# Layer norm behind a depthwise convolution: the last row tile is summed by TensorE on its own, without passing through the running sums

## The chip, the cores and the metric

The kernel runs on one core of a Trainium2 chip. The metric is the device time of one execution in microseconds (us); before the change the median of three runs was 1219.28 us.

## The reference, cut to what matters

One inference step of a small streaming encoder: 512 frames of a new stream and 64 frames of a running one, 576 columns of 1024 channels, all in f32. The first layer mixes time with a convolution module, the second with attention; each has a feed-forward part. The change lies in the convolution module:

```python
def conv_module(xn, prefix, w_in, b_in, w_dw, b_dw, ln_g, ln_b, w_out, b_out):
    a, gate = jnp.split(xn @ w_in + b_in, 2, axis=-1)
    u = a * jax.nn.sigmoid(gate)
    u_ext = jnp.concatenate([prefix.astype(u.dtype), u], axis=1)
    y = depthwise_conv(u_ext, w_dw) + b_dw          # 31 taps, each channel by itself
    y = jax.nn.silu(layernorm(y, ln_g, ln_b))
    return y @ w_out + b_out, u_ext[:, -CONV_STATE:]

def layernorm(x, g, b):
    mu = jnp.mean(x, axis=-1, keepdims=True)
    xc = x - mu
    y = xc * lax.rsqrt(jnp.mean(xc * xc, axis=-1, keepdims=True) + EPS)
    return y * g + b
```

The layer norm needs, for each frame, the sum of y and of its square over all 1024 channels.

## The kernel before, in words

Channels lie on the 128 partitions, time along the free dimension, so the 1024 channels are eight tiles. A column stretch of y has 608 elements (576 frames and the padding between the two streams).

The eight tiles are convolved in two ways. Tiles 0, 1, 2, 3 and 6 (`ROWS`) are *row tiles*: DVE and ACT with GpSimd apply the 31 taps (`conv`, line 1053); the last addition, line 1089, gives `y`. Tiles 4, 5 and 7 (`POLY`) are *polynomial tiles*: their input is stored to DRAM and read back spread over four phases of time (`vt`, line 935), TensorE multiplies it with band matrices (`wm`, loaded at line 938; the products `py` at line 942), DVE adds bias and shift (`ye`, line 952), and the result goes back through DRAM (lines 959 and 964). They work in the layout "p j n": four phases j of 152 columns n, where time is 4n + j.

The statistics of the layer norm are gathered in one PSUM tile, `cl` (two halves of 152 columns, for sum and sum of squares). For the polynomial tiles a matmul with `sum_of` adds up partitions. For the row tiles DVE keeps two running sums in the phase layout, `ys` of y and `sq` of the square (`add`, line 1095; the square by ACT, line 1101). Since a row tile has time in its natural order, these read y with a step of four floats (`in_phases`, line 1050). When the last row tile has been added, `rows_stat` lets TensorE add each running sum over the partitions with four matmuls with `sum_to`, one for each phase (`stat_rows`, lines 1002 and 998).

From `cl` come the square of the mean (`vs`, ACT, line 1211), the variance (DVE, lines 1212 and 1214), the negated mean `nmp` (ACT, line 1196), logarithm and exponential for the reciprocal root (`rs`, lines 1215 and 1216), and a Newton step on DVE that gives `rp` (lines 1217 to 1223). TensorE spreads mean and root over all partitions and back into the order of time (`nm` and `rt`, matmuls with `row_of`, line 1205). ACT copies `nm` for GpSimd (`nms`, line 1279). Then each tile is normalised: y plus mean (`zf`, line 1248), times root (line 1256), SiLU on ACT twice (`zh` rounded, line 1266, and in f32, line 1260), the rest `zl` (line 1270); the products `po` with the output weights follow (line 604). The output weights come by loads of 512 KB on SP's queue (`wr`, line 317). Matmuls of ones on nothing that is used (`warm`, line 794) keep TensorE's clock up in between; fourteen of them stand ahead of the layer norm's end.

The whole convolution module is one section of a planner (`Plan`, line 113). The code hands it operations in some order with an engine, an estimated cost, and what each reads and writes; it lists them by longest remaining path, with a preference for those marked urgent, and emits each engine's instructions in the order of the start times it found. So an edit of a few operations can move instructions of other engines, far from the edit.

Of the kernel before, what the change touches and what calls it, by code (L numbers as in the profile page):

```python
# [6 lines left out]
AF = mybir.ActivationFunctionType  # L7
# [3 lines left out]
P = 128  # L11
# [16 lines left out]
YW = UW - CS  # L28
# [11 lines left out]
QW = QN - Q0  # L40
# [9 lines left out]
ROWS = tuple(c for c in range(8) if c not in POLY)  # L50

KN = ROWS[:2]
# [60 lines left out]
class Plan:  # L113
# [19 lines left out]
    def op(self, eng, cost, fn, reads=(), writes=(), lat=0.0, group=None, bias=0.0, urgent=False, port=False):  # L133
        i, deps = len(self.ops), set()
        for k in reads:
            if k in self.w:
                deps.add(self.w[k])
            self.r.setdefault(k, []).append(i)
        for k in writes:
            deps.update(self.r.pop(k, ()))  # L140
            if k in self.w:
                deps.add(self.w[k])
            self.w[k] = i
        deps.discard(i)
        self.ops.append((eng, cost, fn, deps, lat, group, bias, urgent, port or eng == "Pool"))
        self.end.append(0.0)
# [75 lines left out]
def build(tc, xT, vec, st, stp, bdp, wt, ck, cv, w_in, w_out, gu, down, wk, wv, wq, wo, yT, csp, css, kp, ks, vp, vs):  # L222
    nc = tc.nc
# [88 lines left out]
    X = {}  # L312
# [32 lines left out]
    op = plan.op  # L345
# [8 lines left out]
    def tile(key, tag, shape, dt=F32, pool=None):  # L354
        X[key] = (pool or cur[0]).tile(list(shape), dt, name="_".join(map(str, key)), tag=tag)
        return X[key]
# [4 lines left out]
    def act(n, scaled=True):  # L361
        return 0.186 + n * 0.000834 if scaled else 0.16 + n * 0.000715

    def dve(n, ptr=False):
        return n / 960 + (0.13 if ptr else 0.07)
# [256 lines left out]
    class Norm:  # L622
# [7 lines left out]
        def add(self, c, e="Pool"):  # L630
            self.add_to(int(c == NC - 1), c in (0, NC - 1), c, e)
# [370 lines left out]
    def stat_rows(x, dep, i):  # L1002
        stat([((lambda j=j: sum_to[:, 96 - 32 * j : 224 - 32 * j]), (lambda j=j: x()[:, j, :])) for j in range(Q)], [dep], i)
# [46 lines left out]
    def in_phases(t):  # L1050
        return t.rearrange("p (n j) -> p j n", j=Q)
# [52 lines left out]

    def rows_sums(c):

        rows_done.append(c)
        a = rows_done[0]
        if c in KN[2:]:
            add(("ys",), "ys", ("y", c), ("y", c), True)  # L1110
        elif c == KN[1]:
            op("DVE", dve(YW), lambda: nc.vector.tensor_tensor(tile(("ys",), "ys", (P, Q, QW)), in_phases(X[("y", a)]), in_phases(X[("y", c)]), op=ALU.add), reads=[("y", a), ("y", c)], writes=["ys"], port=True)
        if c not in KN:
            add(("ys",), "ys", ("y", c), ("y", c), True)
            square(c)
        if c == ROWS[-1] and c not in KN:
            rows_stat()

    def rows_stat():
        a = ROWS[0]  # L1120
        stat_rows(lambda: X[("ys",)], "ys", 0)
        stat_rows(lambda: X[("sq", a)], "ysq0", 1)
# [45 lines left out]
    for e in events:  # L1168
        c = int(e[1:] or 0)
# [14 lines left out]
    def small(key):  # L1184
        return tile((key,), key, (P, QW))
# [26 lines left out]
    op("DVE", dve(QW, True), lambda: nc.vector.scalar_tensor_tensor(X[("vs",)], cl(1), 1.0 / D, X[("vs",)], op0=ALU.mult, op1=ALU.subtract), reads=sts, writes=["vs", "cl"], urgent=True)  # L1212
    op("ACT", act(QW) + 0.2, mean, reads=sts, writes=["nmp", "cl"], urgent=True)
    op("DVE", 0.08 + QW / 1920, lambda: nc.vector.tensor_scalar(X[("vs",)], X[("vs",)], 0.0, EPS, op0=ALU.max, op1=ALU.add), writes=["vs"], urgent=True, port=True)
    op("ACT", act(QW), lambda: nc.scalar.activation(small("rs"), X[("vs",)], AF.Ln), reads=["vs", "tbl"], writes=["rs"], urgent=True)
    op("ACT", act(QW), lambda: nc.scalar.activation(X[("rs",)], X[("rs",)], AF.Exp, scale=-0.5), reads=["tbl"], writes=["rs"], urgent=True)
    op("DVE", dve(QW), lambda: nc.vector.tensor_tensor(X[("vs",)], X[("vs",)], X[("rs",)], op=ALU.mult), reads=["rs"], writes=["vs"], urgent=True, port=True)
    op("DVE", dve(QW, True), lambda: nc.vector.scalar_tensor_tensor(X[("vs",)], X[("vs",)], -0.5, X[("rs",)], op0=ALU.mult, op1=ALU.mult), reads=["rs"], writes=["vs"], urgent=True, port=True)
# [1275 lines left out]
```

## Time and profile before

| | |
|---|---|
| median of 3 runs | 1219.28 us (1218.8 to 1220.41) |
| the profiled execution's own time | 1219.93 us |
| its span, first to last instruction | 1218.2 us |
| busy share of PE, DVE, ACT, GpSimd | 98%, 83%, 82%, 66% |
| granted TensorE clock | 0.995 of full speed |
| chain that ended last | PE 71%, DVE 11%, POOL 3%, issue 2%, ACT 2% |

Times in the profile count from the start of the span. PE is TensorE, DVE VectorE, ACT ScalarE, POOL GpSimd, SP the queue that sends the DMAs. A row of a timeline has the start, the length, the engine, the line, what is written and read, the shape, how many instructions are merged, and in brackets how long the engine stood idle before it and what ended that. An f32 matmul has two records in the trace.

### The profile page before, as it was taken

The page shows a single profiled execution, that of the slowest core. Times are in us where ns is not written, and L with a number is a line of the kernel's source. Part 1 is how long each engine was busy: PE and PEld are TensorE (multiplying, and loading weights), DVE is VectorE, ACT ScalarE, POOL GpSimd, SP SyncE. Part 2 cuts the span into 40 slices and gives each one's busy share as a digit, 9 for nine tenths or more (in the row PEclk, how much of TensorE's full clock was granted, in tenths as well). Part 3 has the DMA queues.
Part 4 walks back from the last instruction along what each step waited for, and adds up shares of the span by engine and source line. Part 5 has one row for each costly group of instructions (what it writes and reads, how often), then busy time and mean ns, then how long its engine had stood idle before and what let it go on. Part 6 is the DMA issues. An engine that isn't in the chain of part 4 may idle for free.

```text
span 1218.2 us, 23815 instructions
## 1 busy us (share of the span) xinstructions
PE 1190.0 (98%) x8670; PEld 1161.4 (95%) x8670; DVE 1016.9 (83%) x1643; ACT 998.1 (82%) x1887; POOL 808.6 (66%) x644
## 2 busy tenths in 40 slices
PE   9999989999999999999999999998999999999996
PEld 8999989999999999999999888998999999999996
DVE  6999987979996765998679999979799966668995
ACT  7988474799888887988659999955998889889983
POOL 1999823597867876996204554454699677789951
PEclk9999999999999999999999999999999999999998
DMA  7333822123133323323364322132232424224212
GB/s 270 90 94 93 263 67 86 52 92 117 53 122 105 104 70 94 115 70 106 118 160 105 74 62 74 53 104 59 81 121 71 121 71 122 87 70 123 86 70 78
DMA packets 44997, 121.07 MB, mean 99 GB/s; under 512 B 8784, under 2 KB 14224, under 8 KB 44880
## 3 DMA queue, kind: packets, MB, share of 16 engines
q1 hardware_dynamic: 44880, 119.56, 32.4%
q8 instruction: 68, 1.11, 0.4%
q14 instruction: 49, 0.40, 0.1%
HBM read 105.18 MB, written 5.70 MB: 91 GB/s over the span
## 4 chain that ended last, share of the span: by engine, by line
PE 71%; DVE 11%; POOL 3%; issue 2%; ACT 2%; DMA 1%; SPq 0%; DVEq 0%; POOLq 0%; ACTq 0%
PE j_A L1432 29%; PE j_B L1432 15%; PE j_C L1432 7%; PE po L604 4%; PE b L2226 3%; PE pw L604 3%; PE pq L604 3%; DVE wl L528 2%; DVE acc L1065 2%; PE b L2133 1%; PE av L2253 1%; PE pk L604 1%; DMA qd<-qd 1%; PE pd L604 1%; PE pg L604 1%
## 5 line engine op out<-in xcount | busy, mean ns | idle before, releaser
L518 ACT ACTIVATE wh<-wr 128x512 fp32r<-128x512 f32 (+1 forms) x295 | 178.9, 613 | 34.3 <-PE po L604 15.2
L528 DVE TENSOR_TENSOR wl<-S,hp 128x512 fp32r<-128x512 f32 (+1 forms) x258 | 169.4, 662 | 37.7 <-ACT hp L523 35.0
L528 DVE TENSOR_TENSOR wl<-wr,hp 128x512 fp32r<-128x512 f32 (+1 forms) x233 | 154.2, 666 | 43.2 <-ACT hp L523 39.4
L518 ACT ACTIVATE wh<-S 128x512 fp32r<-128x512 f32 (+1 forms) x260 | 155.7, 610 | 8.1 <-PE j_C L1432 2.9
L523 ACT ACTIVATE hp<-S 128x512 fp32r<-128x512 f32 (+1 forms) x258 | 148.6, 580 | 11.0 <-DVE wl L528 6.3
L523 ACT ACTIVATE hp<-wr 128x512 fp32r<-128x512 f32 (+1 forms) x233 | 134.3, 579 | 16.1 <-DVE wl L528 12.4
L448 POOL TENSOR_TENSOR S<-wr,wr 128x512 f32<-128x512 f32 (+1 forms) x65 | 87.7, 1349 | 86.1 <-ACT wh L518 32.1
L1082 POOL TENSOR_TENSOR pacc<-pacc,pr 128x608 f32<-128x608 f32 x69 | 109.0, 1592 | 7.3 <-ACT pr L1079 4.1
L484 POOL TENSOR_TENSOR S<-wr,S 128x512 f32<-128x512 f32 (+1 forms) x65 | 92.1, 1418 | 26.7 <-DVE wl L528 13.4
L448 POOL TENSOR_TENSOR S<-wr 128x512 f32<-128x512 f32 (+1 forms) x65 | 88.4, 1360 | 21.6 <-ACT wh L518 9.0
L448 POOL TENSOR_TENSOR S<-S,wr 128x512 f32<-128x512 f32 (+1 forms) x65 | 91.3, 1406 | 7.3 <-DVE wl L528 6.5
L1609 POOL TENSOR_TENSOR t<-t,r 128x576 f32<-128x576 f32 x44 | 69.0, 1572 | 3.5 <-ACT t L1580 2.3
L1609 POOL TENSOR_TENSOR a<-a,r 128x576 f32<-128x576 f32 x44 | 70.2, 1599 | 1.1 <-DVE a L1586 1.1
L1065 DVE SCALAR_TENSOR_TENSOR acc<-u,vecs,acc 128x608 f32<-128x608 f32 x76 | 64.6, 850 | 1.0
L1079 ACT ACTIVATE pr<-u,vecs 128x608 f32<-128x608 f32 x69 | 54.0, 795 | 8.3 <-POOL pacc L1082 8.0
L1615 DVE TENSOR_TENSOR a<-a,t 128x576 f32<-128x576 f32 x44 | 52.3, 1188 | 8.1 <-ACT t L1613 7.7
L1580 ACT ACTIVATE t<-j_A 128x288 f32<-128x288 f32 x84 | 34.1, 406 | 23.8 <-PE j_A L1432 22.7
L528 DVE TENSOR_TENSOR wl<-wr,wh 128x512 fp32r<-128x512 f32 x62 | 48.8, 797 | 4.1 <-ACT wh L518 4.0
L2226 PE MATMUL b<-s,sums 128*128 128x512 f32 (+1 forms) x196 | 48.4, 357 | 0.0
L1665 DVE TENSOR_TENSOR h<-j_A,h 128x288 f32<-128x288 f32 x92 | 41.2, 450 | 7.0 <-PE j_A L1432 6.6
L1989 POOL COPY qs<-q 128x64 f32<-128x64 f32 x8 | 3.3, 409 | 56.3 <-DVE q L1986 56.3
L1432 PE MATMUL j_A<-('x', 0, 0)_0_b,wh 128*128 128x288 f32 x168 | 35.7, 295 | 0.5 <-ACT wh L518 0.5
(987 smaller groups left out, 4541.0 us busy)
## 6 DMA issues: line engine op xcount, KB each, us to landing
wr<-gu SPq DMA_DIRECT2D x88, 512.0 KB, 3.6
wr<-down SPq DMA_DIRECT2D x32, 512.0 KB, 3.8
wr<-w_in SPq DMA_DIRECT2D x15, 512.0 KB, 3.9
wm<-wt SPq DMA_DIRECT2D x12, 576.0 KB, 6.3
wr<-down SPq DMA_DIRECT2D x16, 384.0 KB, 3.2
qd<-qd SPq DMA_DIRECT2D x21, 256.0 KB, 2.9
wr<-w_out SPq DMA_DIRECT2D x8, 512.0 KB, 3.8
wr<-wq SPq DMA_DIRECT2D x8, 512.0 KB, 3.6
```

The lines of the kernel that those rows point to most:

```text
L448: eng(e).tensor_tensor(t[:, :n], x[1](), y[1](), op=ALU.subtract if sub else ALU.add)
L484: eng(e).tensor_tensor(v[:, :n], X[("raw", i0)][:, n : 2 * n], v[:, :n], op=ALU.subtract)
L518: nc.scalar.activation(X[("w", u)][0][:, :n], get(), AF.Copy)
L523: nc.scalar.activation(t[:, :n], get(), AF.Copy)
L528: eng(le).tensor_tensor(b[:, :n], get(), a.bitcast(F32)[:, :n], op=ALU.subtract)
L604: nc.tensor.matmul(o[hf], (hi, hi, lo)[j][:, s], (xh, xl, xh)[j], start=(start and q == 0 and j == 0), stop=(stop and q == n - 1 and j == ...
L1065: nc.vector.scalar_tensor_tensor(dst, src, wt_, dst if i else X[("kneg",)], op0=ALU.mult, op1=ALU.add)
L1079: nc.scalar.activation(tile(("pr", c, i), f"pr{m}", (P, YW)), src, AF.Copy, scale=wt)
L1082: nc.gpsimd.tensor_tensor(X[("pacc", c)], X[("pacc", c)], X[("pr", c, i)], op=ALU.add)
L1432: nc.tensor.matmul(out, a[:, s], b, start=(start and q == 0 and i == 0), stop=(q == len(ops_) - 1 and i == 2), skip_group_check=True,)
L1609: nc.gpsimd.tensor_tensor(X[k], X[k], r, op=ALU.mult)
L2226: nc.tensor.matmul(out(zz()), X[(w,)], get(x), start=False, stop=(i == len(mms) - 1), skip_group_check=True)
```

## The change

When the last row tile (6) comes, the running sums of the four earlier row tiles are handed to TensorE as they are. Tile 6 gets eight matmuls of its own: four on y, whose operand is y read with a step of four floats, and four on its square, which ACT now writes in the natural order of time (contiguous in and out, marked urgent), read with the same step by TensorE. DVE's two additions for tile 6 are gone. Besides, the planner is told that the logarithm waits for the mean.

```diff
     def rows_sums(c):
 
+        if c == ROWS[-1] and c not in KN:
+            rows_stat()
+            stat_rows(lambda: in_phases(X[("y", c)]), ("y", c), 0)
+            op("ACT", act(YW, False), lambda: nc.scalar.activation(tile(("sq", c), "ysq1", (P, YW)), X[("y", c)], AF.Square), reads=[("y", c)], writes=["ysq1"], urgent=True)
+            stat_rows(lambda: in_phases(X[("sq", c)]), "ysq1", 1)
+            return
         rows_done.append(c)
...
-        if c == ROWS[-1] and c not in KN:
-            rows_stat()
...
-    op("ACT", act(QW), lambda: nc.scalar.activation(small("rs"), X[("vs",)], AF.Ln), reads=["vs", "tbl"], writes=["rs"], urgent=True)
+    op("ACT", act(QW), lambda: nc.scalar.activation(small("rs"), X[("vs",)], AF.Ln), reads=["vs", "nmp", "tbl"], writes=["rs"], urgent=True)
```

Lines after the edit count four more in the changed kernel than before. Behind the convolution module the order of every engine is as it was; within it the planner moves instructions on all engines. Three places matter.

On PE, the sums `cl` between the products of the last polynomial tile and the spreading of the mean. Before (`yes`, and the first `sq` with `sum_of`, are the sums of tiles 4 and 5; `ye_7` and `sq_7` those of tile 7; `ys` and `sq_1143` the running sums of the row tiles):

```order
L998 MATMUL cl<-yes,sum_of 128x152
L998 MATMUL cl<-sq_1737,sum_of 128x152
L998 MATMUL cl<-ye_7_0_1876,sum_of 128x152
L998 MATMUL cl<-sq_7_0_1882,sum_of 128x152
L794 MATMUL warm<-ones 128x128 x2
L998 MATMUL cl<-ye_7_1_1895,sum_of 128x152
L794 MATMUL warm<-ones 128x128 x2
L998 MATMUL cl<-sq_7_1_1908,sum_of 128x152
L794 MATMUL warm<-ones 128x128 x2
L998 MATMUL cl<-ys,sum_to 128x152 x4
L998 MATMUL cl<-sq_1143,sum_to 128x152 x4
L794 MATMUL warm<-ones 128x128 x8
```

The same place on PE in the changed kernel (`y_1900` is tile 6, `sq_1910` its square, `sq_1151` the running sum of squares):

```order
L998 MATMUL cl<-yes,sum_of 128x152
L998 MATMUL cl<-ys,sum_to 128x152 x4
L998 MATMUL cl<-sq_1151,sum_to 128x152 x4
L998 MATMUL cl<-y_1900,sum_to 128x152 x4
L998 MATMUL cl<-sq_1910,sum_to 128x152 x4
L998 MATMUL cl<-sq_1735,sum_of 128x152
L998 MATMUL cl<-ye_7_0_1876,sum_of 128x152
L998 MATMUL cl<-sq_7_0_1882,sum_of 128x152
L998 MATMUL cl<-ye_7_1_1896,sum_of 128x152
L998 MATMUL cl<-sq_7_1_1908,sum_of 128x152
L794 MATMUL warm<-ones 128x128 x7
```

The sums of the row tiles now stand ahead of five sums of the polynomial tiles, and seven of the fourteen warming matmuls are left ahead of `nm`; the other seven stand behind `rt`.

On SP's queue, around the moment when the input of tile 7 is read back (`vt_1735`, `vt_1738`) and its bands are loaded (`wm`). Before:

```order
L938 DMA wm_2_1685<-wt 128x1152
L938 DMA wm_1_1701<-wt 128x1152
L959 DMA dy_1710<-ye_1703 128x304
L910 DMA csp<-so_1676 128x30
L910 DMA css<-so_1676 128x30
L935 DMA vt_1735<-du_1638 32x4x160
L938 DMA wm_3_1740<-wt 128x1152
```

The same place on SP's queue in the changed kernel:

```order
L938 DMA wm_1_1687<-wt 128x1152
L938 DMA wm_2_1703<-wt 128x1152
L959 DMA dy_1710<-ye_1679 128x304
L317 DMA wr_1727<-w_out 128x1024
L935 DMA vt_1738<-du_1638 32x4x160
L938 DMA wm_3_1743<-wt 128x1152
```

A load of output weights stands there instead of two small stores; before, that load was sent behind the second store of tile 5's result, and the two stores stand there now.

On DVE, the first steps of the normalising stage (`zf_1968` is tile 0 and `zf_1978` tile 1). Before:

```order
L1248 TENSOR_TENSOR zf_1968<-y_735,nm 128x512
L1248 TENSOR_TENSOR zf_1968<-y_735,nm 128x64
L1256 TENSOR_TENSOR zf_1968<-rt_1962,zf_1968 128x288
L1248 TENSOR_TENSOR zf_1978<-y_1039,nm 128x512
L1248 TENSOR_TENSOR zf_1978<-y_1039,nm 128x64
L1256 TENSOR_TENSOR zf_1968<-rt_1963,zf_1968 128x288
```

The same steps on DVE in the changed kernel (`zf_1963` is tile 0, `zf_1970` tile 1):

```order
L1252 TENSOR_TENSOR zf_1963<-y_741,nm 128x512
L1252 TENSOR_TENSOR zf_1963<-y_741,nm 128x64
L1252 TENSOR_TENSOR zf_1970<-y_1039,nm 128x512
L1252 TENSOR_TENSOR zf_1970<-y_1039,nm 128x64
L1260 TENSOR_TENSOR zf_1963<-rt_1961,zf_1963 128x288
L1260 TENSOR_TENSOR zf_1963<-rt_1962,zf_1963 128x288
```

Tile 1's addition has moved ahead of the first product of tile 0.

## The prediction

> **What bounds the kernel now.** I began with the page's busy times, then cut the program into stretches at the place of the change.
>
> ```profile
> span 1218.2 us, 23815 instructions
> PE 1190.0 (98%) x8670; PEld 1161.4 (95%) x8670; DVE 1016.9 (83%) x1643; ACT 998.1 (82%) x1887; POOL 808.6 (66%) x644
> 100.00:150.00 50.00, 48.10 (x364) 47.55 (x363) 49.05 (x69) 32.08 (x47) 48.31 (x37) 1.00 0.65 196
> 150.00:160.00 10.00, 9.75 (x80) 9.28 (x78) 6.35 (x15) 4.15 (x8) 0.00 (x0) 1.00 0.34 80
> 160.00:171.00 11.00, 7.70 (x53) 6.62 (x52) 10.68 (x28) 10.18 (x14) 7.69 (x7) 1.00 0.16 48
> 171.00:200.00 29.00, 29.00 (x215) 28.79 (x216) 19.02 (x34) 18.14 (x30) 3.19 (x3) 1.00 0.30 92
> ```
>
> The last four rows give, after the length, the busy time of PE, weight loads, DVE, ACT and POOL, the granted clock, the DMA share and GB/s. The average says TensorE. The stretches say more: from 100 to 150 us the convolution's taps keep DVE busy 49.05 of 50. From 150 to 160 no engine is really the limit: PE's 9.75 holds its warming matmuls, and a dependent chain passes between engines. From 171 us on PE works without a gap (29.00 of 29), so what this change moves before that point should be carried to the end, one for one.
>
> The chain of waits gives that passage in order (start, length, what):
>
> ```profile
> 151.42 0.70 DVE y L1089
> 152.12 0.22 DVE sq L1021
> 152.34 1.18 DVE ys L1095
> 153.57 2.33 PE cl L998 x16
> 155.90 1.78 PE warm L794 x16
> 157.69 1.76 PE nm L1205 x16
> ```
>
> The last row tile is ready, DVE adds it to the running sum, then PE sums over the partitions. The second addition, of the squares, hides behind the first sums. The end of the passage is set by PE's warming matmuls and `nm`, not by the variance. The timelines of PE, ACT and DVE complete it:
>
> ```profile
> 137.98 12.06 PE L942 MATMUL py<-vt,wm 128*128 128x152 f32 x90 [1.63 <-DMA wm<-wt]
> 149.88 0.42 PE L998 MATMUL cl<-yes,sum_of 128*128 128x152 f32 x2
> 150.13 0.42 PE L998 MATMUL cl<-sq,sum_of 128*128 128x152 f32 x2
> 153.57 1.30 PE L998 MATMUL cl<-ys,sum_to 128*128 128x152 f32 x8 [0.20 <-DVE ys L1095]
> 154.71 1.20 PE L998 MATMUL cl<-sq,sum_to 128*128 128x152 f32 x8
> 155.74 1.95 PE L794 MATMUL warm<-ones 128*128 128x128 f32 x16
> 157.52 1.93 PE L1205 MATMUL nm<-nmp,row_of 128*128 128x72 f32 x16
> 159.29 1.95 PE L1205 MATMUL rt<-rp,row_of 128*128 128x72 f32 x16
> 161.62 0.40 PE L604 MATMUL po<-zh,wh 128*128 128x288 f32 x1 [0.38 <-ACT zh L1266]
> ...
> 155.94 0.30 ACT L1211 ACTIVATE vs<-cl 128x152 f32<-128x152 f32 x1 [2.46 <-PE cl L998]
> 157.13 0.34 ACT L1196 ACTIVATE nmp<-cl 128x128 f32<-128x128 f32 x2
> ...
> 156.27 0.32 DVE L1212 SCALAR_TENSOR_TENSOR vs<-cl,vs 128x152 f32<-128x152 f32 x1 [1.97 <-ACT vs L1211]
> 158.42 0.38 DVE L1223 SCALAR_TENSOR_TENSOR rp<-vs,rs 128x128 f32<-128x128 f32 x2
> 159.49 0.82 DVE L1248 TENSOR_TENSOR zf<-y,nm 128x512 f32<-128x512 f32 x2 [0.69 <-PE nm L1205]
> 161.08 0.82 DVE L1248 TENSOR_TENSOR zf<-y,nm 128x512 f32<-128x512 f32 x2 [0.25 <-ACT nms L1279]
> ```
>
> An f32 matmul shows as two passes. The starts 149.88 and 150.13 give 0.255 us for a matmul of 152 columns, 1.03 for four (154.71 to 155.74).
>
> **The sum, part by part.**
>
> *Removed on the path.* DVE's two additions go, and the slow square with them. That looks like 1.4 us: PE need not wait until 153.57, only for y at 152.12 and a hop of 0.05 (as from 153.53 to 153.57 in the chain), 152.17.
>
> *Added on PE.* Eight more matmuls, 2.04 us. The order shows where: behind the first sum of the polynomial tiles PE takes the old running sums, then the new tile, and five sums of the polynomial tiles, which ran early before, now stand last. Step by step, with strided reads taken as free: `ys` and `sq` start at 150.13 and take 2.06, until 152.19; the new tile until 153.22; its square (ready at 152.16 + 0.70, by the contiguous squares below, 152.86) until 154.25; five sums of 0.255 until 155.53. Before, that point was 155.74. So of the apparent 1.4 us **0.21** is left; the rest goes to the five sums (1.28).
>
> *Mean before logarithm.* ACT would start `vs` at 155.73 and DVE at 156.06, until 156.38. The mean then runs in ACT's gap and is ready near 156.8 rather than 157.47. It isn't what `nm` waits for: seven warming matmuls stand ahead, 14 passes of 0.111 (16 from 155.74 to 157.52), until 157.08. `nm` starts there instead of at 157.52, **0.44** earlier in all, with `rp` ready in time (158.80 before) for `rt`, which follows `nm` by 1.77 (157.52 to 159.29), so at 158.85. The logarithm now queues behind the mean on ACT; DVE lets both go at about the same moment, so that is 0.1 at most, and `nm` hides it. DVE's first normalising addition follows `nm`, so it too is 0.44 earlier.
>
> *The normalising stage.* The same additions and products stand in another order: tile 1's addition goes ahead of tile 0's first product. That is 0.73 later for tile 0, less the wait of 0.25 shown at 161.08, and seven warming matmuls now stand between `rt` and the first output product: `rt` is issued until 160.62 (again 1.77), the warming ones (14 of 0.111) until 162.2, 0.6 later than 161.62. Behind it PE has 3.3 us of waits up to 171 (11.00 less 7.70) to take that in. I count **0**, with 0.5 either way.
>
> *The strided reads.* The new matmuls read y and its square with a step of four floats. No matmul of the trace reads so; other engines do:
>
> ```profile
> L1101 ACT ACTIVATE sq<-y x5: 1289/1317/1322, 83.4 to 152.2; 128x608 f32<-128x608 f32 x5
> L1028 ACT ACTIVATE sq<-ye x2: 692/702/711, 132.0 to 142.0; 128x608 f32<-128x608 f32 x2
> 152.26 1.25 DVE L1095 TENSOR_TENSOR ys<-ys,y 128x608 f32<-128x608 f32 x1
> 153.51 0.79 DVE L1095 TENSOR_TENSOR sq<-sq,sq 128x608 f32<-128x608 f32 x1
> ```
>
> In each pair the first row reads y with that step, the second is contiguous (ns, then us). The step costs ACT (1317 - 702) / 608 = 1.01 ns an element and DVE (1250 - 790) / 608 = 0.76. On 16 passes of 152 that would be 2.46 or 1.84 us, all on the path, since the passes stand one behind another. Lower end: nothing, if PE, which spends 0.85 ns an element in a pass (0.129 / 152), fetches that slowly anyway. A gain is excluded, since nothing else in the pass changes. Upper end: all of ACT's row, 2.17 ns an element, 0.33 a pass, +3.2 us. Both engines that read so pay, so I take the middle of the two, **+2.15**. The Trainium skill (SBUF — State Buffer, section "Door 1: The DMA port swizzle") speaks against the change here: accesses to one 16-byte line run at full bandwidth, and every crossing to a new line is penalised; the trace agrees on ACT and DVE, and no run here shows PE. By its half-sentence that four fp32 may be stepped over for free, the sum would lose this term; ACT's 1317 against 702 speaks against that reading.
>
> *A load that moves.* One 512 KB load of the output weights now stands on SP's queue ahead of the spread of tile 7's input (`vt`) and its bands (`wm`). The queue's timeline and two stretches:
>
> ```profile
> 128.70 0.33 SPq L959 DMA_DIRECT2D dy<-ye  x1
> 129.59 0.44 SPq L910 DMA_DIRECT2D css<-so  x1
> 130.12 0.38 SPq L935 DMA_DIRECT2D vt<-du  x1
> 130.56 1.50 SPq L938 DMA_DIRECT2D wm<-wt  x2
> 144.64 0.38 SPq L317 DMA_DIRECT2D wr<-w_out  x1
> 128.00:130.00 2.00, 2.00 (x18) 2.00 (x17) 1.90 (x5) 0.80 (x1) 1.91 (x2) 1.00 1.04 405
> 134.00:136.00 2.00, 2.00 (x18) 2.00 (x17) 2.00 (x3) 0.37 (x1) 2.00 (x1) 1.00 0.97 367
> ```
>
> With the engines full (1.04, 0.97), 512 KB at 405 to 367 GB/s are 1.3 to 1.4 us, and PE already waited for a band until 137.98; from there to the sums it has no gap, so a delay goes straight to the end. Against it: two small stores and the store of `ye` leave that place or go sooner, so `vt` and the band can be sent up to 0.8 us earlier than 130.12. Between 0 (no gain: y is not ready before 152.17 anyway) and 1.4 I take **+0.4**.
>
> Sum: -0.44 + 0 + 2.15 + 0.4 = **+2.1 us**. The profiled execution took 1219.93, 0.65 over the median of the runs, 1219.28; it would become 1222.0, the median **1221.4**. About 0.2%, 2.4 us, can be told from no change here.
>
> **The rivals.**
>
> *The step is free on PE.* For it: the 0.85 ns an element, slow enough for a memory with half the rate. Against it: ACT pays, whose contiguous row is hardly slower an element (702 / 608 = 1.15 with its fixed part). Then -0.44 + 0.4 = 0: 1219.2.
>
> *The load lands in front, in full, and it is slower.* Place: SP's queue at 129 us; price 1.4 us, decisive with the stride paid from 0.7 on (-0.44 + 2.15 + 0.7 = 2.4). For it: full DMA engines and a PE that waits for that band. Against it: the earlier sending. -0.44 + 2.15 + 1.4 = 3.1: 1222.4.
>
> *The change does what it seems to say*, and the end of the stage comes forward: 1.4 us and 0.2 of the mean, 1217.7. Against it stands PE's order, with five sums behind the new tile; only if PE were far ahead of y could it be, and it reaches it at 152.19 against 152.17.
>
> **How the numbers follow.** Forecast 50%, free step 30%, the load in front 15%, the gain 5%. In the forecast the step's price of 1.84 to 2.46 with 0.5 around it and the load's 0 to 0.7 reach from +1.2 to +2.9, with about a third above 2.4. So slower by over 0.2%: 0.16 + 0.13 = 0.29. Faster by over 0.2% needs more than any case gives; 0.04 for the end of the gain case. Same: 0.67. The likeliest case's own range is 1220.5 to 1222.2; the free step and the load in front widen it to 1218.5 to 1222.9.
>
> **What would show it.** The passes of `cl<-y` and of the last `cl<-sq` at the rows of `sum_to`: a spacing of about 0.26 us is the paid step, 0.13 the free one. The five `sum_of` matmuls stand behind them. The wait before `py` (137.98) tells the load's delay, and the start of `nm` against that of the last sum the warming. I am wrong if `nm` starts before 157.0 or after 161, or if PE shows gaps past 171 us.

## The result, and the profile after

The changed kernel takes 1221.1 us (median of 17 runs, 1217.76 to 1222.53), the kernel before on the same chips 1218.09 us (17 runs, 1217.5 to 1220.41). The ratio of the two, taken over all runs, is 1.0019 with a 95% interval of 1.0013 to 1.0026: 2.3 us slower, between 1.6 and 3.2 (the medians alone lie 3.0 us apart). The forecast was 1221.4 us and +2.1 us.

The page of the changed kernel, as busy times of the engines:

```profile
span 1218.5 us, 23843 instructions
PE 1192.5 (98%) x8686; PEld 1162.7 (95%) x8686; DVE 1021.4 (84%) x1641; ACT 997.3 (82%) x1887; POOL 805.2 (66%) x644
```

Sixteen PE records more (eight matmuls) and two DVE instructions fewer, as the diff says. The stretches of the changed kernel, with the columns as in the prediction:

```profile
100.00:150.00 50.00, 48.56 (x369) 48.14 (x369) 49.06 (x68) 31.62 (x46) 47.88 (x34) 1.00 0.65 194
150.00:160.00 10.00, 9.44 (x59) 8.23 (x58) 3.07 (x10) 3.01 (x8) 0.00 (x0) 1.00 0.31 71
160.00:171.00 11.00, 9.46 (x71) 8.53 (x70) 10.28 (x25) 7.09 (x11) 5.49 (x5) 1.00 0.17 48
171.00:200.00 29.00, 28.28 (x207) 27.84 (x208) 20.68 (x37) 19.50 (x30) 2.92 (x3) 1.00 0.29 92
```

Up to 150 us DVE remains the limit, busy 49.06 of 50 us. From 150 to 160 us DVE's time has halved (6.35 to 3.07), while PE has fewer records (59 for 80) in nearly the same time (9.44 for 9.75): each takes longer. And PE, which worked 29.00 of 29 us behind 171 us, now works 28.28. The prediction had named gaps there as a sign that it is wrong; they are explained below.

PE's timeline of the changed kernel at the place of the change:

```profile
148.77 0.42 PE L998 MATMUL cl<-yes,sum_of 128*128 128x152 f32 x2
149.03 1.20 PE L998 MATMUL cl<-ys,sum_to 128*128 128x152 f32 x8
150.06 1.20 PE L998 MATMUL cl<-sq,sum_to 128*128 128x152 f32 x8
151.81 2.41 PE L998 MATMUL cl<-y,sum_to 128*128 128x152 f32 x8 [0.56 <-DVE y L1089]
154.04 2.35 PE L998 MATMUL cl<-sq,sum_to 128*128 128x152 f32 x8
156.22 0.44 PE L998 MATMUL cl<-sq,sum_of 128*128 128x152 f32 x2
...
157.27 0.42 PE L998 MATMUL cl<-sq,sum_of 128*128 128x152 f32 x2
157.53 1.72 PE L794 MATMUL warm<-ones 128*128 128x128 f32 x14
159.09 1.90 PE L1209 MATMUL nm<-nmp,row_of 128*128 128x72 f32 x16
160.82 1.95 PE L1209 MATMUL rt<-rp,row_of 128*128 128x72 f32 x16
162.61 1.77 PE L794 MATMUL warm<-ones 128*128 128x128 f32 x14
164.14 0.38 PE L604 MATMUL po<-zh,wh 128*128 128x288 f32 x1
```

The two groups of eight passes on the running sums, which lie contiguous, start 1.03 us apart (149.03, 150.06): 0.129 a pass. The two on tile 6 start at 151.81 and 154.04 and end with the start at 156.22: 4.41 us for sixteen passes, 0.276 a pass. The five `sum_of` matmuls stand behind them, seven warming matmuls follow, then `nm`.

DVE, and ACT, of the changed kernel in the same stretch:

```profile
150.98 0.78 DVE L1089 TENSOR_TENSOR y<-acc,pacc 128x608 f32<-128x608 f32 x1
158.06 0.32 DVE L1216 SCALAR_TENSOR_TENSOR vs<-cl,vs 128x152 f32<-128x152 f32 x1 [6.07 <-ACT vs L1215]
161.03 1.55 DVE L1252 TENSOR_TENSOR zf<-y,nm 128x512 f32<-128x512 f32 x4 [0.55 <-PE nm L1209]
164.90 2.39 DVE L1274 TENSOR_TENSOR zl<-zf,zh 128x288 fp32r<-128x288 f32 x2
...
151.79 0.71 ACT L1110 ACTIVATE sq<-y 128x608 f32<-128x608 f32 x1 [0.60 <-DVE y L1089]
157.72 0.30 ACT L1215 ACTIVATE vs<-cl 128x152 f32<-128x152 f32 x1 [5.22 <-PE cl L998]
```

DVE now stands idle for 6.07 us where it had its additions, and ACT for 5.22: both wait for PE. Tile 6 is ready at 150.98 + 0.78, 0.36 us earlier than before.

To carry this to the end, I set each DVE instruction of the changed kernel beside the same one of before, counted from the end of the program, and subtracted the starts (us):

```
before at      191    240    300    400    470    590    600   1100
changed      +2.15  +2.17  +2.27  +2.21  +2.24  +1.80  +0.38  +0.36
```

What was lost by 191 us is still lost at 470 us. By 590 us 0.4 of it has gone; the large step, 1.4 us, comes between 590 and 600 us, and not by the change: the profiled execution of before had half the granted clock there for 3.4 us (0.50 in the second of these stretches),

```profile
588.98:592.39 3.41, 1.95 (x13) 1.48 (x12) 3.41 (x7) 3.41 (x7) 1.69 (x4) 1.00 0.31 44
592.39:595.80 3.41, 3.41 (x16) 3.41 (x16) 3.08 (x5) 3.41 (x7) 0.36 (x1) 0.50 0.97 387
```

which the profiled execution of the changed kernel did not:

```profile
592.00:596.00 4.00, 2.75 (x18) 2.52 (x19) 4.00 (x8) 4.00 (x8) 0.54 (x2) 1.00 0.65 219
```

So the two spans, 1218.2 and 1218.5, understate the difference; the shift of 2.15 us at 191 us and the 2.3 us of the ratio agree. In the experiments I therefore read the shift at 191 us, split into three: the start of tile 6's `y` (DVE), from there to the first pass of `nm` (PE), and from `nm` to 191 us, the normalising stage.

### The profile page after: what moved, and what is told of

Its sections match the earlier page's. It is cut to its first block, busy times and chain, and to the rows that moved or that the text cites. A ratio compares the mean times of both kernels' runs of the same rounds, so it can differ in the third digit from the quotient of the medians.

```text
span 1218.5 us, 23843 instructions
## 1 busy us (share of the span) xinstructions
PE 1192.5 (98%) x8686; PEld 1162.7 (95%) x8686; DVE 1021.4 (84%) x1641; ACT 997.3 (82%) x1887; POOL 805.2 (66%) x644
## 4 chain that ended last, share of the span: by engine, by line
PE 74%; DVE 10%; POOL 2%; issue 2%; ACT 2%; DMA 1%; SPq 0%; DVEq 0%; POOLq 0%; ACTq 0%
PE j_A L1436 30%; PE j_B L1436 15%; PE j_C L1436 7%; PE po L604 4%; PE b L2230 3%; PE pw L604 3%; PE pq L604 3%; DVE acc L1065 2%; PE b L2137 1%; PE av L2257 1%; DVE wl L528 1%; DMA qd<-qd 1%; PE pk L604 1%; PE pd L604 1%; PE pg L604 1%
## 5 line engine op out<-in xcount | busy, mean ns | idle before, releaser
L1436 PE MATMUL j_A<-('x', 1, 3)_0_b,wh 128*128 128x288 f32 x168 | 35.9, 295 | 0.0
```

The source lines that it names most:

```text
L1436: nc.tensor.matmul(out, a[:, s], b, start=(start and q == 0 and i == 0), stop=(q == len(ops_) - 1 and i == 2), skip_group_check=True,)
```

## The experiments

**1. The same matmuls, contiguous.** All instructions and their order stay; only the operand of the eight matmuls changes, so tile 6's sums mix the frames and this kernel leaves that part of the layer norm out.

```diff
-            stat_rows(lambda: in_phases(X[("y", c)]), ("y", c), 0)
+            stat_rows(lambda: X[("y", c)].rearrange("p (j n) -> p j n", j=Q), ("y", c), 0)
...
-            stat_rows(lambda: in_phases(X[("sq", c)]), "ysq1", 1)
+            stat_rows(lambda: X[("sq", c)].rearrange("p (j n) -> p j n", j=Q), "ysq1", 1)
```

> The changed kernel, except that the eight matmuls of tile 6 read y and its square in contiguous runs of 152 columns instead of with a step of four. Instructions, order and sizes are the same on every engine; the sums of tile 6 then mix the frames, so that part of the layer norm is not computed. Theory (the step costs 0.279 instead of 0.129 us a pass): the sixteen passes take 2.06 us instead of 4.45, nm starts near 156.7 instead of 159.09, and the kernel is 2.2 to 2.4 us faster than the changed one, about the time of before. Rival (the 2.2 us came from the new order of the normalising stage or from the warming matmuls behind rt): nm starts earlier, but the first products of the output weights and the end stay within 0.5 us. Rival (these passes are slow for another reason than the step): passes stay at 0.279 us, no change.

Measured: 1219.18 us, ratio 1.0008 [0.9999, 1.0017]; shift at 191 us +0.19. PE's timeline of this kernel:

```profile
152.13 1.30 PE L998 MATMUL cl<-y,sum_to 128*128 128x152 f32 x8 [0.21 <-DVE y L1089]
153.26 1.20 PE L998 MATMUL cl<-sq,sum_to 128*128 128x152 f32 x8
154.30 0.42 PE L998 MATMUL cl<-sq,sum_of 128*128 128x152 f32 x2
157.15 1.90 PE L1209 MATMUL nm<-nmp,row_of 128*128 128x72 f32 x16
```

The sixteen passes take 2.17 us (152.13 to 154.30) instead of 4.41, and from `y` (here 151.29) to `nm` 5.86 us instead of 8.11. So the strided read is the loss on the way to `nm`. At 191 us this kernel is 1.96 us ahead of the changed one, less than the 2.2 to 2.4 expected, because its `y` happens to start 0.31 us later.

**2. The five old sums first.** In the order that the planner found, tile 6's eight matmuls are put behind the last other sum; nothing else moves.

```diff
+            order = [i for i in order if i not in self.late]
+            at = max(order.index(i) for i in self.sums if i not in self.late) + 1
+            order[at:at] = self.late
```

> The changed kernel, except that on PE the five sums of the polynomial tiles stand ahead of the eight matmuls of tile 6 again; all other rows on all engines are the same. Theory (the five sums stand on the path): PE spends 0.56 us waiting for y of tile 6 in the changed kernel, so of the 1.28 us of the five sums about 0.7 to 0.8 is won: the last sum ends near 156.8 instead of 157.5, nm near 158.4, and the kernel is 0.7 us faster than the changed one. Rival (the mean and the warming matmuls set nm, not the sums): no change within 0.2 us.

Measured: 1220.8 us, ratio 1.0021 [1.0012, 1.0029]; shift +1.79. PE's timeline of this kernel:

```profile
152.85 2.32 PE L1005 MATMUL cl<-y,sum_to 128*128 128x152 f32 x8
155.00 2.34 PE L1005 MATMUL cl<-sq,sum_to 128*128 128x152 f32 x8
157.16 1.74 PE L801 MATMUL warm<-ones 128*128 128x128 f32 x14
158.73 1.90 PE L1221 MATMUL nm<-nmp,row_of 128*128 128x72 f32 x16
```

From `y` (151.43) to `nm` it takes 7.30 us, 0.81 less than in the changed kernel: the five sums did stand in the way, by what was expected. The times don't show it: the median is 0.3 us under the changed kernel's, the ratio to before 1.0021 for 1.0019, and both differences are less than these measurements tell apart.

**3. The square written in phases.** Experiment 2, with ACT's square written in the layout "p j n" (strided in, contiguous out), so that four of the eight matmuls read contiguously.

```diff
...
-nc.scalar.activation(tile(("sq", c), "ysq1", (P, YW)), X[("y", c)], AF.Square)
+nc.scalar.activation(tile(("sq", c), "ysq1", (P, Q, QW)), in_phases(X[("y", c)]), AF.Square)
...
-            stat_rows(lambda: in_phases(X[("sq", c)]), "ysq1", 1)
+            stat_rows(lambda: X[("sq", c)], "ysq1", 1)
```

> The changed kernel with the five sums first as in the run before this, and the square of tile 6 written by ACT in the phase layout (read with the step by ACT, 1.32 us, then read contiguously by PE); y itself is still read with the step. Complete computation. Theory: y's passes 152.4 to 154.6, the square is ready at 153.1 and hidden, its passes take 1.03 us, the last sum ends near 155.6: 1.9 us faster than the changed kernel, and about the time of before (within 0.5 us of it). Rival (the square on ACT comes too late): the passes of the square wait, gain under 1 us.

Measured: 1219.06 us, ratio 1.0007 [0.9997, 1.0018]; shift +0.56. PE's timeline of this kernel has one group of each price, 2.14 us (152.72 to 154.86) and 1.05 (154.86 to 155.91):

```profile
152.72 2.32 PE L1005 MATMUL cl<-y,sum_to 128*128 128x152 f32 x8
154.86 1.21 PE L1005 MATMUL cl<-sq,sum_to 128*128 128x152 f32 x8
155.91 1.72 PE L801 MATMUL warm<-ones 128*128 128x128 f32 x14
```

From `y` to `nm` it takes 6.18 us, 1.93 less than in the changed kernel and as long as before the change, as expected.

**4. What a step costs.** The four matmuls on y read with steps of 1, 2, 3 and 4 floats, and so do those on the square. This kernel leaves out tile 6's sums.

```diff
...
+            t = X[("y", ROWS[-1])] if not i else X[("sq", ROWS[-1])]
+            return t[:, 0 : 152 * (j + 1)].rearrange("p (n j) -> p j n", j=j + 1)[:, 0, :]
```

> The changed kernel, except that the four matmuls on y of tile 6 read 152 floats with a step of one, two, three and four floats, and the four on its square likewise; the sums of tile 6 are therefore not computed. If the cost is one fetch of a 16-byte line for each element that opens a new line, with two elements of a line coming at full rate: 0.129 us a pass for a step of one and two, more for three, 0.279 for four. Rival (any step but one is slow): 0.279 for two, three and four. Rival (the step does not matter to PE): 0.129 or 0.279 for all four alike.

PE's timeline merges the passes of this kernel:

```profile
151.67 1.74 PE L998 MATMUL cl<-y,sum_to 128*128 128x152 f32 x8 [0.57 <-DVE y L1095]
153.23 1.66 PE L998 MATMUL cl<-sq,sum_to 128*128 128x152 f32 x8
154.71 0.44 PE L998 MATMUL cl<-sq,sum_of 128*128 128x152 f32 x2
```

Its single records start as follows (us; the last two are followed by the next group at 153.228 and 154.706), with the time from a pass to the next:

```
step            1                 2                 3                 4
y    151.670 151.903   152.032 152.168   152.304 152.496   152.698 152.957
sq   153.228 153.377   153.506 153.641   153.776 153.970   154.174 154.433
us per pass 0.129 (2nd)  0.135, 0.136      0.19 to 0.20      0.26 to 0.27
```

A pass reads 152 floats of each partition. At these steps they lie spread over stretches of 38, 76, 114 and 152 times 16 bytes. At 1.75 ns for 16 bytes that is 0.067, 0.133, 0.200 and 0.266 us; together with a floor of 0.129 these are the times measured, within 0.01. A step of two floats is nearly free, and steps of three and four pay for the stretch that they pass over. Up to a step of four, a price for each line of 16 bytes that is touched and a price for each byte passed over give the same sum; only a step of more than four would tell them apart, and no run has one. (Its one execution took 1219.12 us; shift +0.66.)

**5. Nothing strided on PE.** Experiment 3, and DVE copies y into phases in two halves; of the five old sums four stand ahead and the last behind.

```diff
...
+                    nc.vector.tensor_copy(X[("yp", c)][:, 2 * k : 2 * k + 2, :], in_phases(X[("y", c)])[:, 2 * k : 2 * k + 2, :])
...
+            stat_rows(lambda: X[("yp", c)], ["yp0", "yp1"], 0)
```

> The changed kernel, in which PE reads nothing with a step: DVE copies y of tile 6 into the phase layout in two halves (304 elements each, at the 1.93 ns an element of the addition with the step, 0.65 us each), ACT writes the square in the phase layout (1.3 us), and on PE four of the five sums of the polynomial tiles stand ahead of the eight matmuls of tile 6, the last behind them. Complete computation. Theory (PE pays 1.76 ns for each 16-byte line, DVE and ACT pay beside other work): with y ready at 152.1, PE is ready at 152.4, the copies at 152.7 and 153.3; the passes of y end near 153.8, those of the square near 154.8, the last sum near 155.1: nm near 156.7, 2.2 to 2.4 us ahead of the changed kernel, 0.5 to 1 us ahead of the kernel before at 200 us into the span. Rival (the copies on DVE come so late that the detour costs what the step did): the passes of y start after 153.6 and nothing is won on the run with the square alone in the phase layout (nm at 157.5).

Measured: 1216.6 us, ratio 0.9989 [0.998, 0.9998], faster than both kernels; shift -1.63. DVE's and PE's timelines of this kernel:

```profile
152.12 0.79 DVE L1122 COPY yp<-y 128x304 f32<-128x304 f32 x2
...
152.79 1.20 PE L1005 MATMUL cl<-yp,sum_to 128*128 128x152 f32 x8
156.67 1.90 PE L1229 MATMUL nm<-nmp,row_of 128*128 128x72 f32 x16
```

The two copies take 0.79 us together, not the 1.3 that I had counted with. From `y` (151.31) to `nm` it takes 5.36 us, 0.82 less than before the change: this is the gain that handing the last tile to PE can bring. But the shift is 0.8 larger than that, and 1.4 larger than what I expected against the changed kernel (3.78 for 2.2 to 2.4). The normalising stage behind `nm` had become shorter, without an edit there. Experiments 9 and 10 come back to that.

**6. Only the order of mean and logarithm.** The kernel before, with the logarithm waiting for the mean; this alone brings the new order of the first steps of the normalising stage (the order from 170 us on, and the warming matmuls behind `rt`, are not quite those of the changed kernel).

```diff
...
-reads=["vs", "tbl"], writes=["rs"], urgent=True)
+reads=["vs", "nmp", "tbl"], writes=["rs"], urgent=True)
```

> The kernel before with the second part of the change alone: the logarithm waits for the mean. The sums are those of before. Besides the two rows on ACT it brings the new order of the normalising stage (tile 1's addition ahead of tile 0's first product) and one warming matmul behind rt. Theory (the stride alone costs): nm starts 0.2 us earlier than in the kernel before (seven warming matmuls ahead instead of eight), and 200 us into the span it stands between 0.4 us ahead and 0.2 behind the kernel before. Rival (the new order of the normalising stage costs): 1 us or more behind at 200 us.

Measured: 1218.7 us, ratio 1.0004 [0.9996, 1.0013]. From `y` (151.57) to `nm` (157.53) it takes 5.96 us, 0.22 less than before; behind it 0.76 more. But in the profiled execution the granted clock fell for 3.4 us from 163.7 us on, in that very stage, so its trace cannot say what the order costs.

**7. The load moved back.** The changed kernel, with the load of output weights put back behind the second store of tile 5's result on SP's queue.

```diff
+        if self.load in order:
+            order.remove(self.load)
+            order.insert(order.index(self.behind) + 1, self.load)
```

> The changed kernel with the load of output weights back behind the second store of tile 5's result on SP's queue; all else alike. My prediction charged 0.4 us (0 to 1.4) for that load ahead of the spread and the bands of tile 7; the trace shows the products of tile 7 ending earlier than before instead. If the load costs DMA time but is covered: the bands land up to 1.3 us earlier, the last product stays within 0.3 us or comes up to 1 us earlier, PE waits that much longer for y of tile 6, and nm stays at its place within 0.1 us. If it costs on the path: nm earlier by more than 0.3.

One execution, 1222.83 us; shift +2.45. PE's timeline of this kernel:

```profile
149.06 0.42 PE L1006 MATMUL cl<-yes,sum_of 128*128 128x152 f32 x2
152.11 2.40 PE L1006 MATMUL cl<-y,sum_to 128*128 128x152 f32 x8 [0.57 <-DVE y L1097]
```

`y` starts 0.29 us later than in the changed kernel, and all behind it as well; PE waits for it 0.57 us, as it waits 0.56 there. The load is not on the path.

**8. Fewer warming matmuls.** Experiment 5 with six instead of fourteen.

```diff
-N_WARM = (10, 14)
+N_WARM = (10, 6)
```

> As the run with the copies, with six warming matmuls instead of fourteen at the end of the layer norm, all ahead of nm. Theory (the warming matmuls pace nm, 0.22 us each, until the mean is ready 1.25 us behind the last sum): nm 0.2 to 0.3 us earlier than with the copies alone, the first product of the output weights 0.4 to 0.6 us earlier than there, and 0.3 us at 200 us; granted clock unchanged. Rival (the clock falls without them): a stretch of half clock of 3.4 us behind 160 us, 1.7 us lost.

Measured: 1218.27 us, ratio 0.9998 [0.9989, 1.0007]; shift -1.05. From `y` to `nm` 5.22 us, 0.14 less than in experiment 5, and yet 0.6 us later at 191 us and 1.7 us slower in the median. The expectation failed, again behind `nm`. The rival of the fallen clock is not the reason: this profile keeps the full granted clock there.

**9 and 10. GpSimd made to wait.** The one difference between experiments 5 and 8 behind `nm` that is as large as the riddle is a subtraction on DVE, `zl` of tile 0's second half (`zl` is `zf` less `zh`). The instructions of that name between 160 and 170 us, with the shortest, median and longest duration in ns, before the change:

```profile
L1270 DVE TENSOR_TENSOR zl<-zf,zh x2: 444/524/605, 164.4 to 164.7; 128x288 fp32r<-128x288 f32 x2
```

in the changed kernel, with GpSimd's additions of the same stretch:

```profile
L1274 DVE TENSOR_TENSOR zl<-zf,zh x2: 682/1234/1785, 164.9 to 165.5; 128x288 fp32r<-128x288 f32 x2
L1252 POOL TENSOR_TENSOR zf<-y,nms x4: 350/1058/1743, 163.4 to 166.9; 128x512 f32<-128x512 f32 x2, 128x64 f32<-128x64 f32 x2
```

and in experiment 5:

```profile
L1294 DVE TENSOR_TENSOR zl<-zf,zh x3: 458/468/737, 162.5 to 167.5; 128x288 fp32r<-128x288 f32 x2, 128x576 fp32r<-128x576 f32 x1
L1272 POOL TENSOR_TENSOR zf<-y,nms x4: 356/1104/1767, 161.0 to 164.8; 128x512 f32<-128x512 f32 x2, 128x64 f32<-128x64 f32 x2
```

The same instruction takes 1.785 us in the changed kernel and 0.468 in experiment 5. Where it is long, GpSimd's second addition of 512 columns had started first: in the changed kernel at 165.23, the subtraction at 165.51, and it ended 0.32 us behind the addition. In experiment 5 the subtraction started first (163.01, the addition 163.12) and was not held up. The addition took about as long in both kernels (1.74 and 1.77 us, its first like 1.56), each time with a DVE subtraction running as it began. What led to the two orders is a near tie just before: DVE's first `zl` started 0.018 us ahead of GpSimd's addition of 64 columns in both kernels, and yet in the changed kernel the subtraction was the lengthened one (0.682 us, the addition 0.350) and in experiment 5 the addition (0.652, the subtraction 0.458). So the short time of experiment 5 behind `nm` is in part luck. In the profiles of experiments 1, 2, 3, 4, 7 and 8 the subtraction takes 1.79 to 1.81 us, in that of experiment 6 1.57. Theory: these two instructions can't run together here, and where one has clearly started first the other waits. To test it, GpSimd's second addition is held back by an instruction of one column that reads the result of the subtraction; on all other engines the order is the same.

```diff
...
+            if c == ZF_POOL[-1]:
+                last = X[("zt", 0)][1][:, HALVES[1][0] : HALVES[1][0] + 1].bitcast(F32)
+                nc.gpsimd.tensor_tensor(z[:, 0:1], last, last, op=ALU.add)
```

In the changed kernel:

> The changed kernel with one more GpSimd instruction: one column of tile 0's second zl is read before GpSimd's second addition zf<-y,nms of 512 columns, so this addition can't start before DVE's second zl has ended. The sums stay as in the changed kernel, strided reads included. Theory of the collision: in the changed kernel DVE's second zl lasts 1.79 us because GpSimd's addition started 0.27 us ahead of it; with the wait it lasts 0.45 to 0.6 us, everything behind it on DVE comes 1.2 to 1.36 us earlier, and the DVE instructions near 191 us, +2.15 us against before in the changed kernel, come to +0.8 to +1.1 us (GpSimd's later additions may cost up to 0.3). Median about 1219.9 us, ratio to before about 1.0010, 1.2 us under the changed kernel. Rival: the long zl has nothing to do with GpSimd and waits for ACT or for its own operands: it stays near 1.8 us, the shift stays at +2.15 or more, median 1221.1 us or more.

Measured: 1219.26 us, ratio 1.0011 [1.0002, 1.0019]; shift +0.87. The subtractions and GpSimd's additions of this kernel:

```profile
L1284 DVE TENSOR_TENSOR zl<-zf,zh x3: 444/665/741, 164.9 to 170.0; 128x288 fp32r<-128x288 f32 x2, 128x576 fp32r<-128x576 f32 x1
L1262 POOL TENSOR_TENSOR zf<-y,nms x4: 342/957/1586, 163.4 to 167.9; 128x512 f32<-128x512 f32 x2, 128x64 f32<-128x64 f32 x2
```

The stretch behind 171 us in the same kernel:

```profile
171.00:200.00 29.00, 29.00 (x216) 28.79 (x215) 20.40 (x37) 19.45 (x32) 4.14 (x3) 1.00 0.30 92
```

The second subtraction now takes 0.444 us. `y` and `nm` lie where they lay in the changed kernel (within 0.03 us), and 191 us is reached 1.28 us earlier; PE has no gap behind 171 us any more. The median is 1.8 us under the changed kernel's, which is of another series of runs; the ratios to before, 1.0011 for 1.0019, put it at 1.0. The collision is shown, with its price at 191 us.

In the kernel with the copies:

> The kernel with the copies (e5) and the same wait of GpSimd's second addition for DVE's second zl. Theory of the collision: e5's profile showed the fortunate order (second zl 0.47 us), which there hung on some 20 ns; its eleven times spread from 1215.4 to 1219.0 us because some executions drew the other order. With the wait the profile stays as e5's (shift near 191 us -1.3 to -1.7 us), and the times lose their upper group: median 1216.2 us, highest under 1217.7, ratio to before about 0.9984. Rival: the spread has other causes: median 1216.6 us and the same spread as e5, or slower by GpSimd's wait.

Measured: 1216.27 us (1214.97 to 1218.27), ratio 0.9986 [0.9977, 0.9995]: the lowest median of this study, 1.7 us under before. Its profile has the subtraction at 0.445 us and takes from `y` to `nm` 5.32 us and behind that 0.70 less than before. The highest time expected, under 1217.7, was missed: one of eleven runs is above that, at 1218.27, where experiment 5 had four above 1218. The shift, -2.45, went beyond the -1.3 to -1.7 expected, because `y` starts 0.86 us earlier than in experiment 5; from `y` on it is -1.56. The ratios of experiments 10 and 5, 0.9986 and 0.9989, lie within each other's intervals, so a gain of the wait in this kernel is not shown.

**11. The same with six warming matmuls.**

> The kernel with the copies and six warming matmuls instead of fourteen (e8), and the same wait. In e8's profile the second zl lasted 1.79 us, in e5's 0.47. Theory of the collision: that alone made e8 0.6 us later than e5 near 191 us; without it e8's shift of -1.05 becomes -1.9 to -2.4 us, and the median is 1215.9 to 1216.2 us, equal to or up to 0.4 us under the kernel with the copies, fourteen warming matmuls and the wait. Rival: fewer warming matmuls cost time by themselves: about 0.5 us slower than that kernel, shift near -1.0 us.

Measured: 1216.86 us, ratio 0.999 [0.9982, 0.9999]; shift -2.23, `y` to `nm` 5.08 us. Against experiment 8 the wait brought 1.2 us at 191 us and 1.4 in the median, so the collision made up most of that riddle. The shift lies within what was expected, the median above it (1216.86 for 1215.9 to 1216.2). Whether fewer warming matmuls cost anything stays open: the intervals of experiments 10 and 11 overlap, and in this profile the granted clock fell for 3.4 us at 161.7 us.

The kernels with several runs, but for experiments 6 and 11, in whose profiles the clock fell in the normalising stage, in one table (us; the middle columns are read from `y`, so they hold whatever moved `y` itself):

```
                      start of y   y to nm   nm to 191,     y to 191,     median,
                                             to before      to before     ratio
before                  151.34       6.18        0             0            1
changed                 150.98       8.11      +0.58         +2.51        1.0019
1 contiguous            151.29       5.86      +0.56         +0.24        1.0008
2 five sums first       151.43       7.30      +0.58         +1.70        1.0021
3 square in phases      151.30       6.18      +0.60         +0.60        1.0007
5 copies                151.31       5.36      -0.78         -1.60        0.9989
8 copies, six warm      150.70       5.22      +0.55         -0.41        0.9998
9 changed, wait         151.01       8.10      -0.72         +1.20        1.0011
10 copies, wait         150.45       5.32      -0.70         -1.56        0.9986
```

In these kernels with the new order the column "nm to 191" takes two values, about -0.7 and +0.6 (+0.61 and +0.59 in experiments 4 and 7), and which of them goes with the collision alone, whatever the sums look like. Experiments 6 and 11, with the fallen clock, have +0.76 and -1.18. The ratios follow the sum in the next column within 0.9 us, about the width of their intervals. Later stretches can move the shift as well: in experiment 9 it goes from +1.23 at 470 us to -0.36 at 590, which no run here explains.

## Why the prediction was right, step by step

The time was right, 1221.4 for 1221.1, and so was its cause, the strided read. That the two times agree within 0.3 us is partly luck: the forecast counted from 1219.28, the median of three runs, which is 1.2 above the 1218.09 of the later series, and the medians have moved by 3.0 instead of 2.1. Of its five terms three were right, one was wrong, and one hid something that the prediction did not see.

- **The apparent gain that goes to the five sums: right.** PE took the new tile as soon as `y` was there (it waited 0.56 us), and the five sums stood behind. Putting them ahead (experiment 2) gave 0.81 us from `y` to `nm`.
- **`nm` is paced by warming, 0.44 earlier: right in kind, a little large.** With contiguous reads the way from `y` to `nm` became 5.86 for 6.18, 0.32 less (experiment 1).
- **The strided reads, +2.15: right in size.** The spacing gives 4.41 less the 2.06 of sixteen contiguous passes, +2.35; `y` to `nm` with and without the step gives +2.25 (8.11 less 5.86). The middle between the prices on ACT and DVE was near, with some luck: the sum took the step as a surcharge on every element, and on PE a step of two costs almost nothing (experiment 4). The Trainium skill (SBUF — State Buffer, section "Door 1: The DMA port swizzle") says that a line of 16 bytes wants at least two hits to run at full bandwidth; two floats a line took 0.135 us for 0.129, so PE agrees with that. The same sentence's four fp32 for free doesn't hold: a step of four took 0.26 to 0.27.
- **The moved load, +0.4: wrong, it is 0.** The step that failed is "from there to the sums it has no gap, so a delay goes straight to the end": there was no delay, and the changed kernel has a gap ahead of tile 6. SP's queue of the changed kernel shows the load sent first and the input and the band behind it all earlier than before (`vt` from 130.12 to 128.41):

```profile
126.50 0.38 SPq L959 DMA_DIRECT2D dy<-ye  x1
126.98 0.52 SPq L317 DMA_DIRECT2D wr<-w_out  x1
128.41 0.33 SPq L935 DMA_DIRECT2D vt<-du  x1
128.78 2.28 SPq L938 DMA_DIRECT2D wm<-wt  x2
```

  PE's products of the last polynomial tile ended 1.1 us earlier (first sum at 148.77 for 149.88), and PE then waited for `y`, which DVE's taps set. The wait for the band, 1.63 us before, is gone. Experiment 7 with the load moved back waits the same 0.57 us.
- **The normalising stage, 0 with 0.5 either way: the size was just missed (+0.58), and its make-up was not seen.** It is two terms. Without the collision the stage is 0.70 to 0.78 shorter than before (experiments 5, 9, 10); that the new order brings this is argued, not shown, since in experiment 6 the clock fell. The collision of DVE's subtraction with GpSimd's addition costs 1.3 (9 against the changed kernel). The sign that I had named, no gaps on PE behind 171 us, was broken by it: PE waits 0.75 us at 171.59 for an ACT that was late by the subtraction. The prediction counted when instructions are issued, not which two then run at the same time.
- **The sum.** Measured at 191 us: `y` -0.36, `y` to `nm` +1.93, `nm` to 191 +0.58, together +2.15. Predicted: -0.44 + 2.15 on the way to `nm` (+1.71), 0 behind it, +0.4 ahead, +2.1. That these agree within 0.1 is partly luck: 0.8 too much ahead of `y` stands against 0.2 and 0.6 too little behind it. The -0.36 of `y` itself is no effect that I would claim; over the kernels here `y` starts between 150.45 and 151.57.

Of the rivals, the free step falls with experiments 1 and 4, the load in front with experiment 7, and the gain was there to be had only once PE's reads were made contiguous and the collision did not fall (experiments 5 and 10, 1216.6 and 1216.27 us).

## What to carry to other kernels

Before TensorE is given an operand as another engine left it, look at the step with which it would be read: a matmul took twice as long here with a step of four floats and hardly longer with a step of two, while two copies and a square written in phases, on engines that were waiting anyway, cost less than that step. Where a change shifts engines against each other, look for pairs of DVE and GpSimd instructions that newly fall together, since which of them starts first can cost 1.3 us. And split a measured shift at fixed points of the path before explaining it: a total that agrees with the forecast may hide two errors that cancel.

## What the runs showed of the hardware that I had not expected

- A pass of 152 f32 columns on PE costs 0.129 us at a step of one, 0.135 at two, 0.19 to 0.20 at three and 0.26 to 0.27 at four floats (experiment 4): up to this step, the larger of the contiguous time and about 1.75 ns for each 16 bytes passed over.
- A strided DVE copy is far cheaper than a strided DVE addition: 0.79 us for two copies of 304 columns (experiment 5), against 1.25 us for one addition of 608 that reads one of its two operands with the same step (before).
- A DVE subtraction of two SBUF tensors of 288 columns takes 0.444 us alone and 1.785 when a GpSimd addition has started 0.27 us ahead of it; started 0.12 us ahead of the addition it takes 0.468. The addition takes 0.2 us longer than its first like in both cases. Starts within 0.02 us of each other go either way. DVE's additions with one operand in PSUM (`zf<-y,nm`) are not held in this way: they take 0.81 us for 512 and 64 columns together beside GpSimd's additions too (163.95 in the changed kernel, while GpSimd's first addition runs from 163.40 on). The Trainium skill says this of the port that the two engines share (SBUF — State Buffer, section "Who interferes with whom"): a DVE instruction with two SBUF inputs contends with a GpSimd instruction that reads SBUF, the shared port is locked for one of them at a time, and the order of issue decides who is blocked. The trace agrees, with 1.785 us on one side and 0.468 on the other.
- In some profiled executions the granted clock falls to half for 3.4 us, near 590 us (before, experiments 1, 7 and 11) or near 162 us (experiments 6 and 11); in before's it cost 1.4 us (the step from +1.80 to +0.38 in the table of shifts). Each time PE had been busy only in part in the 3.41 us ahead: 1.93 to 1.95 us near 590, 1.92 and 2.30 near 162. The other profiles have such a stretch near 590 too (1.92 to 1.95 of some 3.41 us) and keep the full clock. The Trainium skill (TensorE: Matmul & The Clock Gate, section "What's actually happening") says that the clock is gated by a window of 3413 ns that runs freely, whatever the kernel does, and watches how busy PE is. The traces agree with the length, and the two falls in experiment 11 lie 426.67 us apart, 125 times that length. That section asks for an idle window; here one with PE busy for 56 to 67% of it came ahead of the fall. How busy PE was does not decide it alone: counted in such windows from its own fall, experiment 1 has one that ends at 842.34 us with PE busy for only 1.71 us, and the clock stays full behind it. What decides stays open.
